# A hybrid attention block on one core: conditioning sums two weight tiles at a time, and three selection masks one to three units later

## The chip, the cores and the metric

The kernel runs on one core of a Trainium2 chip. The metric is the device time of one execution in microseconds; the figure given for a kernel is the median of several runs.

## The reference, cut to what matters

One layer of a decoder trunk with 1024 tokens and a width of 1024, all in float32:

```
mod = silu(c) W_ada + b_ada -> (shift1, scale1, gate1, shift2, scale2, gate2)
h   = RMSNorm(x) * (1 + scale1) + shift1
P   = h W_in
mixer A: out_A = u * (tril(W_s[g]) v_chunk + b[g])      # u, v = split(gelu(P_A))
mixer B: 8 query heads x 64, 2 kv heads; a light indexer scores all causal keys,
         the top 256 of them are attended with softmax
o   = concat(RMSNorm(out_A), RMSNorm(out_B)) W_out
x   = x + gate1 * RMSNorm(o)
h2  = RMSNorm(x) * (1 + scale2) + shift2
x   = x + gate2 * RMSNorm(relu(h2 W_1)^2 W_2)
```

`W_ada` is 1024 x 6144. Its first two column groups (shift1, scale1) are summed early in the kernel. The other four groups of 1024 columns are called 2 to 5 in the code: gate1, shift2, scale2 and gate2. Each is a sum over the 1024 inputs, held as eight tiles of 128 x 1024.

## The kernel before, in words

The program is written in stages: projections and the indexer first, then a selection that finds each query block's threshold among its keys, then attention, the output projection, and the feed-forward part. The code gives operations to engines by name and gives each a priority from its place in the program; a planner with a simulated timeline then fixes the order on every engine and the slots of the tile pools, and puts in the waits. Each engine runs its list in order. So an edit to the program's order moves more than the lines that it touches.

The change is in the attention stage, a loop over 32 units `u`. Query blocks of 128 tokens are taken in the order OB = 0, 7, 1, 6, 5, 4, 3, 2, four units to a block (two kv groups, two pairs of heads): units 4 to 7 are block 7, 8 to 11 block 1, 12 to 15 block 6, 16 to 19 block 5, 20 to 23 block 4, 24 to 27 block 3, 28 to 31 block 2. Block b has b + 1 key tiles, so block 1 is short work and block 6 long. In one pass of the loop the program asks for:

- `logits(u + 1)`: matmuls of queries and keys into one of three PSUM buffers (L730), a reduction on VectorE that adds the bias BI and takes the extreme (L731), and the exponential on ScalarE (L734);
- `values(u)`: transposes of the probabilities (L769), their copy by ScalarE (L750), matmuls with the values (L755), and the division by the sums on VectorE (L779, L780);
- `mask(b)` at the units listed in `MASKS`: eleven VectorE operations (L671 to L686), five of them over the block's keys, which turn the scores SC of block b into its bias BI. The mask of block b is needed at the logits of block b;
- `stack_for(u + 3)`: the queries of a coming unit (L322, L391, L392);
- `finish_a(b)` at the third unit of a block (load of the tile `ya`, VectorE L795, transposes L709, copies L712, L713), and `finish(b)` one block later for the other half (L785, L98, L99, L787, again L709 to L713);
- `WO[0] = w_chunk(...)` once: four loads of 512 KB of W_out, eight splits in two parts, on ScalarE (L224) and VectorE (L225);
- from u = 19 at odd u `oproj0`, 24 matmuls of the output projection (L807 to L809);
- `ada_sum(g)`: eight loads of W_ada (L477), and eight VectorE operations on 128 x 1024 that sum them into `adacc` (L479, L481); four units later `ada_use(g)`: sixteen matmuls with a column of ones (L165) and small VectorE operations.

Scores SC and other tiles of the selection live in pools that the loop closes at one unit; a new pool `op_` is opened in their space and holds six of the eight tiles of WO[0]. The ring `wp` has twelve slots of 4 KB a partition, for logits, queries, two tiles of WO[0], W_ada tiles and the sums. All loads named here are issued by SyncE (SP), in order.

Of the kernel before, what the change touches and what calls it, by code (L numbers as in the profile page):

```python
# [9 lines left out]
F32 = mybir.dt.float32  # L10
# [9 lines left out]
P = 128  # L20
# [3 lines left out]
KD = 8  # L24
# [13 lines left out]
def trunk(ctx, tc, x, c, positions, w_ada, b_ada, g_pre_mix, w_in, g_sgu_v, w_spatial, b_spatial,  # L38
# [8 lines left out]
    def nm(s):  # L47
        uid[0] += 1
        return f"{s}_{uid[0]}"
# [9 lines left out]
    wp = ctx.enter_context(tc.tile_pool(name="wp", bufs=12))  # L59
# [12 lines left out]
    def ct(shape, dt, name):  # L72
        return cst.tile(shape, dt, tag=name, name=name)

    def push(name, side="left"):
        st = ExitStack()
        return st, st.enter_context(tc.tile_pool(name=name, bufs=1, side=side, reuse_waits="tile"))
# [84 lines left out]
    def ada_cols(dst, acc):  # L162
        p = p_mm()
        for e in range(8):
            T.matmul(p[:, e:e + 1], acc[:, e * P:(e + 1) * P], ones, start=True, stop=True)  # L165
        V.tensor_copy(dst, p[:, :8])
# [303 lines left out]


    mod2 = ct([P, 32], F32, "mod2")
    def ada_sum(g):
        acc = wp.tile([P, 1024], F32, tag="w", name=nm("adacc"))
        for k in range(KD):
            t = wp.tile([P, 1024], F32, tag="w", name=nm("ada"))
            nc.sync.dma_start(t, w_ada[k * P:(k + 1) * P, g * 1024:g * 1024 + 1024])  # L477
            if k == 0:
                V.tensor_scalar(acc, t, cact[:, 0:1], None, op0=OP.mult)  # L479
            else:  # L480
                V.scalar_tensor_tensor(acc, t, cact[:, k:k + 1], acc, op0=OP.mult, op1=OP.add)  # L481
        return acc

    G2 = ct([P, 8], F32, "G2")
    SH2 = ct([P, 8], F32, "SH2")
# [1 line left out]
    ADA = {}  # L487

    def ada_use(g):
        m = mod2[:, (g - 2) * 8:(g - 2) * 8 + 8]  # L490
        ada_cols(m, ADA[g])
        if g == 3:
            V.tensor_tensor(SH2, m, cols[:, 32:40], op=OP.add)
        elif g == 4:
            V.scalar_tensor_tensor(G2, m, 1.0, cols[:, 40:48], op0=OP.add, op1=OP.add)
            V.tensor_tensor(G2, G2, cols[:, 56:64], op=OP.mult)
        else:
            i, b0, g0 = (0, 24, 76) if g == 2 else (1, 48, 84)
            V.tensor_tensor(gate[:, i], m, cols[:, b0:b0 + 8], op=OP.add)
            V.tensor_tensor(gate[:, i], gate[:, i], cols[:, g0:g0 + 8], op=OP.mult)  # L500
# [147 lines left out]
    def search_rest():  # L648

        V.tensor_scalar(more[:, :6], KDS, 8.0, None, op0=OP.is_gt, op1=OP.add, accum_out=more[:, 6:7])  # L650
        p = p_tr()
        flag = T.matmul(p[:1, :1], more[:, 6:7], ones, start=True, stop=True)
        V.tensor_copy(rest, p[:1, :1])
        with tc.tile_critical():
            r = V.value_load(rest)
            with V.If(r > 0):
                for b in range(2, NB):
                    cnt, sg, kk, tf, kq, lf, top8, kd, th, lo, hi = ST[b]
                    search(BI[:, boff[b]:boff[b] + P * (b + 1)].bitcast(U16), 15, lf, cnt, kd, kk, V.drain)
                V.drain()  # L660
        for b in OB[4:]:
            q_proj(b, flag)
# [3 lines left out]
    def mask(b):  # L666

        n = P * (b + 1)
        cnt, sg, kk, tf, kq, lf, top8, kd, th, lo, hi = ST[b]
        sc = score(b)  # L670
        first = V.tensor_copy(lo, lf)  # L671
        if b < 7:
            after(first, lowest[0])
        V.scalar_tensor_tensor(th, hi, 16, lo, op0=OP.logical_shift_left, op1=OP.bitwise_or)

        V.tensor_tensor(tf, th.bitcast(F32), sg, op=OP.mult)
        lt = BI[:, boff[b]:boff[b] + n]
        eq = up.tile([P, 1024], BF, tag="uv", name=nm("eq"), bufs=3)[:, :n]
        after(first, masked[0])
        V.tensor_scalar(lt, sc, tf, None, op0=OP.is_lt, op1=OP.add, accum_out=cnt)  # L680
        V.tensor_scalar(eq, sc, tf, BIG, op0=OP.is_equal, op1=OP.mult)
        V.tensor_tensor_scan(sc, eq, eq, 0.0, op0=OP.add, op1=OP.max)
        V.tensor_scalar(cnt, cnt, float(TOPK - n), BIG, op0=OP.add, op1=OP.mult)
        V.tensor_tensor(cnt, cnt, sc[:, n - 1:n], op=OP.add)
        V.scalar_tensor_tensor(eq, sc, cnt, eq, op0=OP.is_gt, op1=OP.mult)
        masked[0] = V.scalar_tensor_tensor(lt, lt, -BIG, eq, op0=OP.mult, op1=OP.subtract)  # L686
# [31 lines left out]
    def logits(u):  # L718
        b, grp, pair = units[u]
        ch = chunks(P * (b + 1))  # L720
        bias = BI[:, boff[b]:boff[b] + P * (b + 1)]
        for h2 in range(2):
            h4 = pair * 2 + h2
            h = grp * 4 + h4
            L = wp.tile([P, 1024], F32, tag="w", name=nm("L"))[:, :P * (b + 1)]
            top = 3e38
            for i, (c0, cw) in enumerate(ch):
                pl = p_lg()[:, :cw]
                for q in range(2):
                    T.matmul(pl, QS[b, grp][:, q, h4 * P:(h4 + 1) * P], KS[:, grp, c0:c0 + cw], start=q == 0, stop=q == 1)  # L730
                lowest[0] = V.tensor_tensor_reduce(L[:, c0:c0 + cw], pl, bias[:, c0:c0 + cw], scale=-0.125, scalar=top,  # L731
                                       op0=OP.add, op1=OP.min, accum_out=mxs[:, i, b, h:h + 1])
                top = mxs[:, i, b, h:h + 1]
            ex = A.activation(L, L, AF.Exp, scale=-1.0, bias=top, accum_out=sms[:, b, h:h + 1])  # L734
            after(ex, last_gelu)
            LT[u, h2] = L
# [53 lines left out]
    def finish_a(b):  # L790
        ya = p2.tile([P, 512], F32, tag="yb", name=nm("ya"), bufs=3)
        nc.sync.dma_start(ya, ya_dram[b * P:(b + 1) * P, :])
        V.tensor_tensor(rsa[:, b:b + 1], ssa[:, b, 0:1], ssa[:, b, 1:2], op=OP.add)
        rstd_of(rsa[:, b:b + 1], rsa[:, b:b + 1], 512)
        V.tensor_scalar(ya, ya, rsa[:, b:b + 1], None, op0=OP.mult)  # L795
        merge_T(b, 0, ya)

    def stack_for(u):
        if u < len(units) and units[u][2] == 0:
            b, grp, _ = units[u]  # L800
            QS[b, grp] = q_stack(p2, QT[b], grp, wp.tile([P, 2, 512], F32R, tag="w", name=nm("qs")))
# [22 lines left out]
            return op_.tile([P, 2, 512], F32R, tag="wo", name=nm("wo"), bufs=6)  # L824
        return wp.tile([P, 2, 512], F32R, tag="w", name=nm("wo"))

    MASKS = {4: 6, 6: 5, 8: 4, 9: 3, 10: 2}
    stack_for(0)
    logits(0)
    stack_for(2)  # L830
    for u, (b, grp, pair) in enumerate(units):
        if u == 3:
            at = tc.cur_priority
            tc.cur_priority = 465000
            search_rest()
            mask(7)
            tc.cur_priority = at
        if u + 1 < len(units):
            logits(u + 1)
        values(u)  # L840
        if u in MASKS:
            mask(MASKS[u])
        if u == 12:
            u_stack.close()
            sc_stack.close()
            o_stack, op_ = push("op")
        stack_for(u + 3)
        if u % 4 == 2:
            finish_a(b)
        if u in (24, 28):  # L850
            ada_use(u // 4 - 4)
        if u in (20, 24, 28):
            ADA[u // 4 - 3] = ada_sum(u // 4 - 3)
        if u % 4 == 0 and u:
            finish(OB[u // 4 - 1])
        if u == 14:
            WO[0] = w_chunk(w_out, [(0, 0, 512)], gout, tile_of=wo_tile)
        if u >= 19 and u % 2:
            oproj0(OB[(u - 19) // 2])
# [101 lines left out]
    def bank():  # L961
        nbank[0] += 1
        return BANK[(nbank[0] - 1) % 8]()
# [3 lines left out]
    def ctile():  # L967
        return fc.tile([P, 512], F32, tag="c", name=nm("c"), bufs=4)
# [133 lines left out]
    open_ = None  # L1102
    for pi in range(NF, NP):
        if pi == 5:
            ADA[5] = ada_sum(5)
        if pi == 8:
            ada_use(5)
            gate_rows(g2b, 1)
        w = wparts(pi)
        X, Y, Z = bank(), bank(), bank()  # L1110
        p1, u2, u3 = ctile(), ctile(), ctile()
        f11, f22 = dtile(), dtile()
        chained(X, w, 1, True)
        A.activation(p1, X, AF.Copy)
        if open_:
            ends(*open_)
        chained(X, w, 6, False)
        A.activation(u2, X, AF.Copy)
        chained(Z, w, 2, True)
        V.tensor_tensor(f11, p1, Z, op=OP.add)  # L1120
        relu_sq(f11, f11)
        store_x(1, pi, f11)
        chained(X, w, 7, False)
        A.activation(u3, X, AF.Copy)
        chained(Y, w, 5, True)
        V.tensor_tensor(f22, u3, Y, op=OP.add)
        relu_sq(f22, f22)
        store_x(4, pi, f22)
        open_ = (pi, w, X, Y, u2, f11, f22)
# [164 lines left out]
```

## Time and profile before

| | us |
|---|---|
| median of 3 runs | 1235.24 |
| lowest and highest of these | 1233.52, 1237.39 |
| the profiled execution, device time | 1231.81 |
| its span, first to last instruction | 1229.8 |

The profile lists, for each engine, the instructions in order of time with their durations, and marks before an instruction how long its engine was idle and which engine's work ended that. PE is TensorE's matmuls, PEld its weight loads, DVE VectorE, ACT ScalarE. "PEclk" is the granted clock of TensorE as a share of 2.4 GHz, averaged over a stretch. The attention loop runs from about 290 to 530 us of the span, its last part together with the first half of the output projection.

### The profile page before, as it was taken

To read this page: it belongs to the slowest core of one execution; us is meant where nothing else is said; L and a number is where in the kernel's file an instruction comes from. 1 tells how busy PE (TensorE), PEld (TensorE's weight loads), DVE (VectorE), ACT (ScalarE), POOL (GpSimd) and SP (SyncE) were. 2 spreads that over 40 slices of the span, in tenths; PEclk is the share of its full clock that TensorE was granted. 3 is DMA by queue.
4 is the path that set the end of the run, shared out by engine and by line. 5 is a ranking of instruction groups with operands and counts; after the bars stand their busy time and mean duration, and the time that the engine had idled before them with its cause. 6 is when DMAs were issued, how large, how long until landed. Compare 5 with 4: busy or idle time off the path is not lost.

```text
span 1229.8 us, 16884 instructions
## 1 busy us (share of the span) xinstructions
PE 1156.0 (94%) x5785; PEld 977.9 (80%) x5785; DVE 869.4 (71%) x1798; ACT 671.2 (55%) x1410; POOL 208.6 (17%) x304
## 2 busy tenths in 40 slices
PE   4899989998888999899899999999999999999997
PEld 3888768887687999787678888888887888888885
DVE  6943998995688466628997866565568656877568
ACT  4654669774367655538625555555444544445452
POOL 3585605452100000023600000000000000000001
PEclk9899999998899999899899999999999999999999
DMA  9530202110002044654226754353477365533335
GB/s 335 164 90 24 69 1 61 57 53 23 1 9 81 7 163 163 216 203 156 86 103 222 245 166 154 129 175 121 158 269 297 119 210 170 185 103 88 101 103 205
DMA packets 80240, 162.42 MB, mean 132 GB/s; under 512 B 7724, under 2 KB 32920, under 8 KB 80152
## 3 DMA queue, kind: packets, MB, share of 16 engines
q1 hardware_dynamic: 80136, 161.33, 39.1%
q8 instruction: 45, 0.74, 0.3%
q14 instruction: 43, 0.35, 0.1%
q10 hardware_dynamic: 16, 0.00, 0.0%
HBM read 119.36 MB, written 41.94 MB: 131 GB/s over the span
## 4 chain that ended last, share of the span: by engine, by line
PE 57%; DVE 10%; DMA 3%; issue 2%; ACT 2%; POOL 1%; SPq 0%; DVEq 0%; POOLq 0%; ACTq 0%
PE tr L1174 8%; PE lg L1174 8%; PE mm L1174 6%; PE mm L755 4%; PE lg L991 3%; PE lg L993 3%; PE lg L992 3%; PE tr L991 2%; PE tr L993 2%; PE tr L992 2%; PE mm L993 2%; PE mm L992 2%; PE mm L991 2%; PE tr L769 2%; PE lg L730 2%
## 5 line engine op out<-in xcount | busy, mean ns | idle before, releaser
L881 ACT ACTIVATE w<-rx 128x512 fp32r<-128x512 f32 x112 | 70.6, 631 | 147.5 <-PE lg L1174 63.8
L1174 PE MATMUL tr<-w,w 128*128 128x512 f32 x504 | 134.0, 390 | 2.1 <-DVE w L882 2.1
L1174 PE MATMUL lg<-w,w 128*128 128x512 f32 x504 | 133.8, 390 | 0.0
L882 DVE TENSOR_TENSOR w<-rx,w 128x512 fp32r<-128x512 f32 x112 | 77.1, 688 | 58.6 <-ACT w L881 58.2
L301 PE MATMUL mm<-w,hT 128*128 128x512 f32 (+1 forms) x288 | 111.8, 390 | 4.5 <-ACT hT L293 3.7
L1174 PEld LDWEIGHTS tr<-w,w 128*128 128x128 f32 x504 | 95.1, 189 | 22.3 <-DVE w L882 2.5
L1174 PEld LDWEIGHTS lg<-w,w 128*128 128x128 f32 x504 | 95.0, 189 | 19.8
L304 PE MATMUL mm<-w,hT 128*128 128x512 f32 (+1 forms) x288 | 110.1, 383 | 0.5 <-POOL hT L294 0.5
L303 PE MATMUL mm<-w,hT 128*128 128x512 f32 (+1 forms) x288 | 110.4, 384 | 0.0
L1210 POOL TENSOR_TENSOR rsf<-rsf,mhalf 128x1 f32<-128x1 f32 x8 | 6.0, 751 | 603.2 <-DVE rsf L1209 603.2
L1174 PE MATMUL mm<-w,w 128*128 128x512 f32 x336 | 94.4, 391 | 0.0
L755 PEld LDWEIGHTS mm<-VV,pT 128*128 128x128 f32 x576 | 73.7, 195 | 5.2 <-ACT pT L750 3.4
L755 PE MATMUL mm<-VV,pT 128*128 128x64 f32 x576 | 74.8, 273 | 2.0 <-ACT pT L750 2.0
L1174 PEld LDWEIGHTS mm<-w,w 128*128 128x128 f32 x336 | 63.2, 188 | 13.2
L882 DVE TENSOR_TENSOR w<-b,w 128x512 fp32r<-128x512 f32 x96 | 65.6, 684 | 3.4 <-ACT w L881 3.3
L301 PEld LDWEIGHTS mm<-w,hT 128*128 128x128 f32 x288 | 55.2, 192 | 14.0 <-ACT hT L293 3.9
L734 ACT ACTIVATE L<-L,mxs 128x128 f32<-128x128 f32 (+7 forms) x64 | 49.2, 770 | 28.3 <-DVE mxs L731 28.3
L882 DVE TENSOR_TENSOR w<-s,w 128x512 fp32r<-128x512 f32 x56 | 38.2, 687 | 36.7 <-ACT w L881 36.7
L881 ACT ACTIVATE w<-b 128x512 fp32r<-128x512 f32 x96 | 59.3, 618 | 6.4 <-DMA b<-in_w_ff_dram 6.2
L304 PEld LDWEIGHTS mm<-w,hT 128*128 128x128 f32 x288 | 54.7, 190 | 10.2 <-POOL hT L294 1.0
L730 PE MATMUL lg<-KS,qs 128*128 128x512 f32 (+5 forms) x192 | 52.2, 384 | 10.7 <-DVE mxs L731 5.7
L303 PEld LDWEIGHTS mm<-w,hT 128*128 128x128 f32 x288 | 55.2, 192 | 8.3
(356 smaller groups left out, 2964.6 us busy)
## 6 DMA issues: line engine op xcount, KB each, us to landing
rx<-x_scratch SPq DMA_DIRECT2D x56, 512.0 KB, 3.5
x_scratch<-d SPq DMA_DIRECT2D x108, 256.0 KB, 3.0
ada<-in_w_ada_dram SPq DMA_DIRECT2D x48, 512.0 KB, 5.7
raw<-in_w_ff_dram SPq DMA_DIRECT2D x32, 512.0 KB, 4.2
b<-in_w_ff_dram SPq DMA_DIRECT2D x32, 512.0 KB, 4.5
x<-in_x_dram SPq DMA_DIRECT2D x16, 512.0 KB, 5.8
raw<-in_w_in_dram SPq DMA_DIRECT2D x8, 512.0 KB, 3.6
raw<-in_w_in_dram SPq DMA_DIRECT2D x16, 256.0 KB, 2.9
```

The costliest lines, as they stand in the source:

```text
L301: mm = T.matmul(p[:, :n], lh, wt[k][:, 0, :n], start=k == 0, stop=False)
L303: T.matmul(p[:, :n], lh, wt[k][:, 1, :n], start=False, stop=False)
L304: T.matmul(p[:, :n], ll, wt[k][:, 0, :n], start=False, stop=k == KD - 1)
L730: T.matmul(pl, QS[b, grp][:, q, h4 * P:(h4 + 1) * P], KS[:, grp, c0:c0 + cw], start=q == 0, stop=q == 1)
L734: ex = A.activation(L, L, AF.Exp, scale=-1.0, bias=top, accum_out=sms[:, b, h:h + 1])
L755: mm = T.matmul(po[:, o:o + 64], e[:, (si * 2 + h2) * P:(si * 2 + h2 + 1) * P], VV[:, s0 + si, grp], start=first, stop=pair == 1 and s0 + ...
L881: A.activation(hi, src, AF.Copy)
L882: eng.tensor_tensor(lo, src, hi.bitcast(F32), op=OP.subtract)
L991: ms.append(T.matmul(p, a[:, 0, k], b[:, 0, k], start=start and k == 0, stop=False, skip_group_check=more))
L992: ms.append(T.matmul(p, a[:, 0, k], b[:, 1, k], start=False, stop=False, skip_group_check=more))
L993: ms.append(T.matmul(p, a[:, 1, k], b[:, 0, k], start=False, stop=stop and k == 3, skip_group_check=more))
L1174: ms.append(T.matmul(p, x[:, qa, t * P:(t + 1) * P], y[:, qb], start=start and n == 0, stop=stop and n == 2, skip_group_check=more))
```

## The change

Two things are edited. `MASKS` asks for the masks of blocks 4, 3 and 2 after units 9, 12 and 13 instead of 8, 9 and 10. As the scores are then needed longer, the pools of the selection close (and `op_` opens) after unit 14 instead of 12, and WO[0] is asked for at unit 15 instead of 14.

`ada_sum` becomes `ada_part(g, ks)`, which loads and sums only the tiles `ks`. In the loop, groups 2, 3 and 4 are summed two tiles a unit, in units 19 to 22, 23 to 26 and 27 to 30; before, all eight tiles were asked for at units 20, 24 and 28. `ada_use(2)` and `ada_use(3)` move from units 24 and 28 to 23 and 27. The sums of groups 2 to 4 share one slot in `op_`; before, each took a slot of `wp`. Group 5, summed in the feed-forward part, stays as it was. The number of operations and bytes is unchanged.

```diff
-    def ada_sum(g):
-        acc = wp.tile([P, 1024], F32, tag="w", name=nm("adacc"))
-        for k in range(KD):
+    def ada_part(g, ks):
+        if g not in ADA:
+            ADA[g] = (wp if g == 5 else op_).tile([P, 1024], F32, tag="w", name=nm("adacc"), bufs=12 if g == 5 else 1)
+        acc = ADA[g]
+        for k in ks:
             t = wp.tile([P, 1024], F32, tag="w", name=nm("ada"))
             nc.sync.dma_start(t, w_ada[k * P:(k + 1) * P, g * 1024:g * 1024 + 1024])
             if k == 0:
                 V.tensor_scalar(acc, t, cact[:, 0:1], None, op0=OP.mult)
             else:
                 V.scalar_tensor_tensor(acc, t, cact[:, k:k + 1], acc, op0=OP.mult, op1=OP.add)
-        return acc
...
-    MASKS = {4: 6, 6: 5, 8: 4, 9: 3, 10: 2}
+    MASKS = {4: 6, 6: 5, 9: 4, 12: 3, 13: 2}
...
-        if u == 12:
+        if u == 14:
             u_stack.close()
             sc_stack.close()
             o_stack, op_ = push("op")
         stack_for(u + 3)
         if u % 4 == 2:
             finish_a(b)
-        if u in (24, 28):
-            ada_use(u // 4 - 4)
-        if u in (20, 24, 28):
-            ADA[u // 4 - 3] = ada_sum(u // 4 - 3)
+        if u in (23, 27):
+            ada_use((u - 23) // 4 + 2)
+        if 19 <= u < 31:
+            ada_part((u - 19) // 4 + 2, range((u - 19) % 4 * 2, (u - 19) % 4 * 2 + 2))
         if u % 4 == 0 and u:
             finish(OB[u // 4 - 1])
-        if u == 14:
+        if u == 15:
             WO[0] = w_chunk(w_out, [(0, 0, 512)], gout, tile_of=wo_tile)
...
         if pi == 5:
-            ADA[5] = ada_sum(5)
+            ada_part(5, range(KD))
```

## Rows read from the trace of the kernel before

**Rows 1.** The page: busy time, share of the span and instructions of two engines.
```profile
PE 1156.0 (94%) x5785; PEld 977.9 (80%) x5785; DVE 869.4 (71%) x1798; ACT 671.2 (55%) x1410; POOL 208.6 (17%) x304
```
**Rows 2.** Stretches: length, busy PE, PEld, DVE, ACT, POOL (instructions), clock, DMA share, GB/s.
```profile
355.40:370.00 14.60, 11.34 (x82) 10.63 (x81) 12.91 (x43) 7.98 (x22) 1.77 (x3) 0.88 0.00 0
370.00:396.00 26.00, 22.33 (x167) 19.53 (x166) 23.30 (x65) 20.07 (x39) 1.90 (x3) 1.00 0.24 72
396.00:420.00 24.00, 23.52 (x201) 23.09 (x201) 13.65 (x46) 17.47 (x36) 1.77 (x3) 1.00 0.11 34
420.00:506.40 86.40, 86.40 (x594) 78.70 (x594) 54.32 (x122) 45.64 (x108) 4.23 (x7) 1.00 0.47 171
506.40:511.00 4.60, 1.18 (x10) 0.91 (x8) 4.60 (x9) 4.43 (x10) 0.00 (x0) 1.00 0.16 59
511.00:518.00 7.00, 7.00 (x24) 6.09 (x25) 3.97 (x7) 2.49 (x5) 0.00 (x0) 0.51 0.50 151
```
**Rows 3.** Timeline of PE around 361 us: start, length, line, [idle before].
```profile
360.88 0.50 PE L730 MATMUL lg<-KS,qs 128*128 128x256 f32 x2 [0.35 <-DVE mxs L731]
364.30 1.09 PE L709 MATMUL tr<-ident,yb 128*128 128x128 f32 x4 [2.91 <-DVE yb L787]
...
368.21 0.60 PE L769 MATMUL tr<-ident,L 128*128 128x128 f32 x4
```
**Rows 4.** Timeline of DVE there: the mask of block 4, and the row L787.
```profile
358.80 0.88 DVE L680 TENSOR_SCALAR_CACHE_REDUCE BI<-SC,self 128x640 bf16<-128x640 f32 x1
...
359.61 0.55 DVE L681 TENSOR_SCALAR eq<-SC,self 128x640 bf16<-128x640 f32 x1
...
361.15 1.48 DVE L682 TENSOR_TENSOR_SCAN SC<-eq 128x640 f32<-128x640 bf16 x1
...
362.87 0.88 DVE L685 SCALAR_TENSOR_TENSOR eq<-SC,self,eq 128x640 bf16<-128x640 f32 x1
363.67 0.48 DVE L787 TENSOR_SCALAR yb<-yb,rsb 128x512 f32<-128x512 f32 x1
364.06 0.82 DVE L686 SCALAR_TENSOR_TENSOR BI<-BI,eq 128x640 bf16<-128x640 bf16 x1
```
**Rows 5.** The tiles wo: matmuls and splits, ns min/median/max, first and last start.
```profile
L807 PE MATMUL mm<-wo,mT x64: 387/393/774, 421.1 to 535.6; 128*128 128x512 f32 x64
...
L224 ACT ACTIVATE wo<-raw,cols x8: 707/712/723, 382.7 to 392.3; 128x512 fp32r<-128x512 f32 x8
L225 DVE SCALAR_TENSOR_TENSOR wo<-raw,cols,wo x8: 739/747/1097, 383.7 to 394.4; 128x512 fp32r<-128x512 f32 x8
```
**Rows 6.** Timeline of PE around 509 us.
```profile
506.72 0.82 PE L769 MATMUL tr<-ident,L 128*128 128x128 f32 x6
510.96 1.11 PE L709 MATMUL tr<-ident,ya 128*128 128x128 f32 x4 [3.42 <-DVE ya L795]
```
**Rows 7.** Timeline of DVE there.
```profile
502.72 3.92 DVE L481 SCALAR_TENSOR_TENSOR adacc<-ada,cact,adacc 128x1024 f32<-128x1024 f32 x3
...
506.89 1.27 DVE L481 SCALAR_TENSOR_TENSOR adacc<-ada,cact,adacc 128x1024 f32<-128x1024 f32 x1
...
508.56 1.28 DVE L481 SCALAR_TENSOR_TENSOR adacc<-ada,cact,adacc 128x1024 f32<-128x1024 f32 x1
509.76 0.74 DVE L225 SCALAR_TENSOR_TENSOR w<-raw,cols,w 128x512 fp32r<-128x512 f32 x1
510.43 0.48 DVE L795 TENSOR_SCALAR ya<-ya,rsa 128x512 f32<-128x512 f32 x1
```
**Rows 8.** The W_ada tiles of 420 to 530 us: issues, waits, landing.
```profile
L477 SPq DMA_DIRECT2D ada<-in_w_ada_dram x24: 327/371/740, 431.6 to 499.3; - x24
...
  DMA ada<-in_w_ada_dram: 3.1, 3
...
DMA to landing us min/median/max: 3.7/5.9/7.5
```
**Rows 9.** Timeline of PE: the first twelve of one ada_use's sixteen matmuls.
```profile
468.28 1.45 PE L165 MATMUL mm<-ones,adacc 128*128 128x1 f32 x12
```

## What bounds the kernel now, and what the change should do to it

> **What bounds the kernel now.** The page's first part comes first: the matmul row of TensorE is busy for 94% of the span, VectorE for 71% [rows 1]. Such a kernel ends when TensorE has done its list, so only two things can make it shorter: gaps in TensorE's row, and time at the lower of its two clock levels. The 40 slices point to the attention loop, and the view by stretches shows where in it [rows 2]. From 355.4 to 370 us (the tail of block 7 and block 1) TensorE is idle for 14.60 - 11.34 = 3.26 us, and the mean granted clock is 0.88. With levels of 1.2 and 2.4 GHz that mean says that 24% of the stretch, 3.5 us, ran at half speed, which cost about 1.75 us. From 370 to 396 (block 6) it is idle for 3.67 us at full clock; from 396 to 420 (block 5) for 0.48; from 420 to 506.4 for nothing, though VectorE has 32 us free there. Then 3.42 us idle in 506.4 to 511, and 7.00 us at a clock of 0.51, so about 3.4 us lost: 6.8 us together.
>
> Then the timelines, for what ends those gaps. The first big one, 2.91 us, ends with VectorE's L787 of `finish(7)` [rows 3]. VectorE was never idle: L787 stands behind the scan and L685 of block 4's mask [rows 4]. After that gap four transposes take 1.09 us, and only at 368.21 are they back at 0.60 [rows 3]: this is the low clock. The second gap, 3.42 us, ends with L795 of `finish_a(2)` [rows 6], and before L795 VectorE did five steps of the sum of group 4 and a weight split with hardly a pause [rows 7]. So in both places TensorE waits for a short VectorE operation that stands in line behind long ones nobody needs yet. From 370 to 396 VectorE is busy for 23.30 of 26.0 us [rows 2]; eight splits of WO[0] are part of that [rows 5].
>
> **The change part by part.** Nothing is removed or added: 24 sums, 24 loads and five masks stay. All that moves is place, so every term below is a share of idle time that exists now. The profiled execution took 1231.8 us (span 1229.8, and 2.0 around it), 3.4 under the median of 1235.2; the gain is worked out on the first and taken off the second.
>
> *Block 1's stretch.* The mask of block 4 costs 0.88 + 0.55 + 1.48 + 0.88 + 0.82 = 4.6 us for its five long steps [rows 4] and some 0.8 more for six small ones. It is asked for one unit later, behind `finish(7)`. The mask of block 3 (0.8 of the keys) leaves the stretch; its first three long steps fell into it, by scaling 0.8 x 2.91 = 2.3 us, and some small ones, about 3 together. VectorE then has 12.91 - 3 = 9.9 us of work here, and TensorE needs 11.34 - 1.75 = 9.6 at full clock. Ends: no gain at all (block 4's mask of 5.4 us is still one burst amid short units) and 14.6 - 9.9 = 4.7 us. I take the middle, **2.4**, as the burst stays but its victim `finish(7)` is gone.
>
> *Block 6's stretch.* In come 3 us of block 3's mask, out go the eight VectorE splits, 8 x 0.747 = 6.0 us [rows 5]: 23.3 + 3 - 6 = 20.3 us of VectorE against 22.3 of TensorE [rows 2]. It fits in sum, but both masks stand in the first half. Ends 0 and 3.67; I take half, **1.8**.
>
> *Block 5's stretch.* WO[0]'s splits, one unit later, fall mostly into it: ScalarE 17.47 + 8 x 0.712 = 23.2 us of 24.0, VectorE 13.65 + 6.0 = 19.7 [rows 2, 5]. ScalarE's copies feed the values' matmuls, so a nearly full ScalarE will show. Ends: nothing, and 2.9 us, most of the idle time that block 6 has with these splits now. I take **-1.5**. The loads of WO[0] on SP move with it, behind the `ya` load of unit 14 as before; first use is at unit 19, and the last split now starts at 394.4 and the first matmul with these tiles at 421.1 [rows 5], so a shift of a unit costs nothing there.
>
> *Units 19 to 27.* Two sums a unit, 2.6 us at most, in a stretch where VectorE has 32 of 86 us free [rows 2]: no gain and no loss; the cover is that free time. What is new here are two waits. First, loads come in twelve pairs instead of three sets of eight. Three sets cost VectorE 3.1 us of waiting for a landing [rows 8]; twelve would cost 12, still inside the free time. Behind a wait for a load stand L731 of the next logits, and TensorE behind that. On SP the pairs stand between the `ya` loads and the stores of `oproj0`, and an issue that waits for a slot of `wp` holds these up. Sums no longer take slots there, and at most a few W_ada tiles are open at once, so I count nothing for it. Second, the sums of groups 2 to 4 share one slot: the first sum of group 3 must wait until sixteen L165 matmuls have read group 2, and likewise for 4. Twelve of them take 1.45 us [rows 9]; L731, L780 and L713 queue behind. TensorE has a unit's worth of values and 24 matmuls of `oproj0` to go on with, so again nothing in the sum, with 0 as one end and the last rival's price as the other.
>
> *The end of the loop.* At unit 30 two sums stand where five stood before L795: 3 x 1.28 = 3.8 us less ahead of it [rows 7], more than the gap of 3.42 [rows 6]. If the gap goes the low clock goes with it. Ends 0 and 6.8; VectorE may put other early work there, as it did with the split L225 [rows 7], so I take **5.0**. What is late next is `finish(2)`, whose transposes have `oproj0` and stage 8's projection to cover them; the later stages just start earlier.
>
> Sum: 2.4 + 1.8 - 1.5 + 5.0 = **7.7 us**. The profiled execution would come to 1224.1, the median to 1235.2 - 7.7 = **1227.5**.
>
> **The rivals.**
>
> *The masks only move their stall* (blocks 1 and 6 give nothing, block 5 costs 1.5): for it, VectorE is the full engine from 355 to 396 and its work there hardly shrinks; against it, the rows show one victim, not a lack of capacity. 5.0 - 1.5 = 3.5 us: 1231.7.
>
> *The end keeps its gap*, since what stands before L795 is decided by the planner, which already put a stage-8 split there [rows 7]. Only 2.7 us are won: 1232.5.
>
> *Everything comes back*: 4.7 + 3.7 + 6.8 = 15.2 us, 1220.0. For it, all the gaps have one cause; against it, bursts of 4 to 5 us remain.
>
> *Spread gaps keep the clock low.* Instead of one gap of 2.9 us, TensorE gets several short ones, and half speed remains. In this trace gaps of 3.67 us in all, none with a fall behind it, left the clock at 1.00 from 370 to 396 [rows 2], which speaks against it. Price: the 1.75 us of block 1 stay and block 6 loses as much: 7.7 - 3.5 = 4.2 us, 1231.0. The Trainium skill (TensorE: Matmul & The Clock Gate, section "A second HAM failure mode: psum-queue depth-cycling") describes this: frequent short idles between groups of matmuls make the clock swing. The trace so far doesn't agree.
>
> *Slower: the shared slot of the sums.* At units 23 and 27 VectorE stands at the first sum of the next group until TensorE, which is behind in its own list, has reached L165. If that lasts longer than what TensorE can do without VectorE (the values of one unit and an `oproj0`), TensorE runs dry and its clock falls, as around 509 us: 6.8 us each time, 13.6 for two. 13.6 - 7.7 = 5.9 us slower: 1241.1. Against it: TensorE has no gap at all there now and the wait is a few us.
>
> **How the numbers follow.** Forecast 0.40 (own range 1223 to 1231), stall moved 0.19, end stays 0.13, everything 0.09, clock 0.05, slower 0.14. Faster by over 0.3% (3.7 us, about what a measurement of this kernel can tell from no change) is below 1231.5: the forecast, "everything", half of "stall moved", half of "clock": 0.40 + 0.09 + 0.095 + 0.025 = 0.61. Slower 0.14, the rest, 0.25, is the same. The range from 1220 to 1238 leaves out the slower case and half of "everything".
>
> **What would show it.** Right: no gap over 2 us before L709 in block 1 and at the end, full clock in both places, and VectorE's busy share near even from 420 to 510. Block 5's term: ScalarE's L750 ending gaps in TensorE just after WO[0]'s loads. Wrong: a gap of 3 us or more with a fall of the clock anywhere from 356 to 530, above all one that ends with L481, L479 or L165 (the shared slot or late loads), or a new one ahead of L795. If the time is the same and TensorE's idle time has shrunk, it was given back behind the loop, in stage 8, where VectorE and ScalarE lead.

## The result and the profile after

The changed kernel took **1225.41 us** (median of four executions, 1224.78 to 1229.68), the kernel before 1234.38 beside it: a ratio of **0.9939, 95% interval 0.9918 to 0.9961**. Run again as an experiment below, it gave 0.9955 [0.9938, 0.9972]. By these two ratios the change is worth some 5.5 to 7.5 us; 7.7 were forecast, and 1225.41 is 2.1 below the predicted 1227.5.

The profiled execution of the changed kernel is the slowest of its four, 1229.68 with a span of 1227.9. Its busy times [rows 1] are the same work:

```profile
PE 1156.1 (94%) x5785; PEld 977.7 (80%) x5785; DVE 870.3 (71%) x1798; ACT 671.3 (55%) x1410; POOL 210.9 (17%) x304
```

The view by stretches, with the columns of [rows 2]:

```profile
355.00:370.00 15.00, 12.06 (x98) 11.02 (x98) 12.26 (x36) 8.26 (x23) 2.43 (x3) 1.00 0.00 0
370.00:396.00 26.00, 25.93 (x208) 24.83 (x206) 25.58 (x78) 21.90 (x43) 1.78 (x3) 1.00 0.08 18
396.00:420.00 24.00, 22.77 (x181) 21.68 (x182) 15.14 (x44) 18.52 (x38) 1.78 (x3) 1.00 0.29 93
...
450.00:480.00 30.00, 28.26 (x181) 25.27 (x179) 16.53 (x33) 12.25 (x30) 1.78 (x3) 0.94 0.43 139
480.00:506.00 26.00, 24.50 (x158) 21.75 (x156) 23.56 (x44) 15.53 (x40) 0.55 (x1) 1.00 0.69 223
506.00:520.00 14.00, 12.47 (x80) 11.14 (x81) 5.94 (x10) 9.70 (x21) 2.29 (x2) 1.00 0.51 156
```

Two numbers come out of each line: TensorE's idle time (length less busy PE), and what the low clock costs, (1 - clock) x length. This holds since half speed for a time T loses T/2 and lowers the mean by as much. From 450 to 480 that is 1.74 idle and 0.06 x 30 = 1.8. The table adds them up for every kernel, idle time + clock.

| profiled execution | 355-370 | 370-396 | 396-420 | 420-480 | 480-520 | lost | loop |
|---|---|---|---|---|---|---|---|
| before | 3.3+1.7 | 3.7+0 | 0.5+0 | 0+0 | 3.4+3.4 | 15.9 | 288.5 |
| after | 2.9+0 | 0.1+0 | 1.2+0 | 1.7+1.8 | 3.0+0 | 10.8 | 283.9 |
| e3_same | 2.9+0 | 0.3+0 | 0.7+0 | 1.7+5.1 | 3.0+1.8 | 15.7 | 287.7 |
| e1_masks_only | 2.9+0 | 0.3+0 | 0.7+0 | 0+0 | 2.6+3.4 | 9.9 | 282.4 |
| e2_sums_only | 3.3+2.7 | 2.9+0.8 | 1.3+0 | 1.7+1.8 | 2.7+0 | 17.1 | 290.7 |
| e4_sums_in_eights | 2.9+0 | 0.4+0 | 0.8+0 | 0.5+1.8 | 3.4+3.4 | 13.1 | 286.5 |
| e5_masks_wo_at_14 | 2.9+0 | 1.5+0 | 0.9+0 | 0+0 | 2.8+1.8 | 10.0 | 283.2 |
| e6_two_slots | 2.9+0 | 0.2+0 | 1.1+0 | 1.7+1.8 | 3.0+3.5 | 14.3 | 287.0 |
| e7_sums_two_earlier | 2.9+0 | 0.4+0 | 1.0+0 | 3.4+6.6 | 4.3+4.8 | 23.3 | 300.3 |
| e8_ya_first | 2.9+0 | 0.3+0 | 0.7+0 | 1.1+1.8 | 4.8+9.6 | 21.3 | 294.6 |
| e9_mask4_only | 2.9+0 | 1.6+1.8 | 0.5+0 | 0+0 | 2.6+3.4 | 12.7 | 285.1 |
| e10_masks32_only | 3.3+1.7 | 1.0+0 | 1.8+3.4 | 0+0 | 3.2+3.4 | 17.6 | 288.9 |
| e11_masks_ya_first | 2.9+0 | 0+0 | 1.2+0 | 0+0 | 3.7+1.7 | 9.5 | 282.6 |
| e12_masks_sums_18 | 2.9+0 | 0.3+0 | 0.9+0 | 0+1.8 | 3.0+3.5 | 12.4 | 284.7 |

"Loop" is read from the timeline of PE: from the end of the idle time that block 7's mask causes (L730 at 315.88 before) to the end of the first one of stage 8 (L904 at 604.33 before). "Loop" less "lost" is 271.3 to 273.6 for all but e7, whose clock stays low past 520. So the list of gaps and falls (spells at the lower clock) accounts for the loop to some 2 us. Idle times repeat to half a microsecond between the two profiles of one program (after, e3_same); the clock's share does not.

Outside the loop, where no edit lies, the profiled executions scatter: against before they are between 2.2 us shorter and 1.2 longer ahead of it, and between 2.1 shorter and 4.4 longer behind it. The profile of after, 4.6 us shorter in the loop, is only 1.9 shorter in its span; that of e1, 6.0 shorter in the loop, is 8.8 shorter. So the ratios of the timed executions, and not one profile, say what a version is worth.

The gaps of the changed kernel, timeline of PE (start, length, what, idle before and its releaser; line numbers are one or two higher than before's):

```profile
363.41 0.63 PE L710 MATMUL tr<-ident,yb 128*128 128x128 f32 x4 [1.84 <-DVE self L684]
...
368.44 1.10 PE L756 MATMUL mm<-VV,pT 128*128 128x64 f32 x8 [0.79 <-ACT pT L751]
...
452.54 0.66 PE L710 MATMUL tr<-ident,ya 128*128 128x128 f32 x4 [1.74 <-DVE ya L796]
...
484.10 0.63 PE L710 MATMUL tr<-ident,ya 128*128 128x128 f32 x4 [0.67 <-DVE ya L796]
...
486.23 0.63 PE L322 MATMUL tr<-ident,qd 128*128 128x128 f32 x4 [0.63 <-DVE mT L714]
...
506.56 0.66 PE L770 MATMUL tr<-ident,L 128*128 128x128 f32 x4 [0.76 <-DVE mT L714]
...
509.64 1.52 PE L756 MATMUL mm<-VV,pT 128*128 128x64 f32 x12 [0.96 <-DVE yb L781]
```

Beside [rows 3], the gap of 2.91 us ahead of block 1's transposes is now 1.84, and the transposes take 0.63 us instead of 1.09: no fall of the clock. Beside [rows 6], the 3.42 us ahead of L709 are gone, and several short gaps stand there, at full clock. The third line is new.

The gap in block 1 shrank in an unforeseen way. Timeline of VectorE, beside [rows 4]:

```profile
361.51 0.88 DVE L681 TENSOR_SCALAR_CACHE_REDUCE BI<-SC,self 128x640 bf16<-128x640 f32 x1
...
362.32 0.55 DVE L682 TENSOR_SCALAR eq<-SC,self 128x640 bf16<-128x640 f32 x1
362.78 0.48 DVE L788 TENSOR_SCALAR yb<-yb,rsb 128x512 f32<-128x512 f32 x1
...
363.24 1.48 DVE L683 TENSOR_TENSOR_SCAN SC<-eq 128x640 f32<-128x640 bf16 x1
```

The planner still starts block 4's mask ahead of `finish(7)`, but the short L788 now goes in before the scan and L686, where before it stood behind both.

The new gap, timeline of VectorE:

```profile
449.49 1.28 DVE L483 SCALAR_TENSOR_TENSOR adacc<-ada,cact,adacc 128x1024 f32<-128x1024 f32 x1
450.68 0.17 DVE L780 RECIPROCAL sms<-sms 128x4 f32<-128x4 f32 x1
450.80 1.28 DVE L483 SCALAR_TENSOR_TENSOR adacc<-ada,cact,adacc 128x1024 f32<-128x1024 f32 x1
452.00 0.48 DVE L796 TENSOR_SCALAR ya<-ya,rsa 128x512 f32<-128x512 f32 x1
```

and what TensorE does behind it:

```profile
453.91 1.84 PE L165 MATMUL mm<-ones,adacc 128*128 128x1 f32 x16
455.61 1.98 PE L756 MATMUL mm<-VV,pT 128*128 128x64 f32 x16
...
458.94 0.63 PE L809 MATMUL mm<-wo,mT 128*128 128x512 f32 x1
...
461.77 0.39 PE L808 MATMUL mm<-wo,mT 128*128 128x512 f32 x1
```

Two sums stand in line ahead of L796 of `finish_a(4)`, though TensorE needs their result only at L165, behind the transposes that wait for L796: the pattern of [rows 7], 58 us earlier in the span. A little later a matmul of 512 columns takes 0.63 us instead of 0.39, the lower clock level.

The gap at the end of the loop went in an unforeseen way too. The last sum ends at 505, but L796 of `finish_a(2)` starts no earlier for it: its load is issued at 507.64 us, where it was 499.71 before, and VectorE waits for that.

```profile
511.87 0.49 DVE L796 TENSOR_SCALAR ya<-ya,rsa 128x512 f32<-128x512 f32 x1 [2.38 <-DMA ya<-ya_scratch]
```

TensorE isn't held up, since its list now has matmuls of `oproj0` there, from 510.97 to 515.40, ahead of the transposes. In e2, e3 and e6 below it is the same.

### The profile page after: what moved, and what is told of

It is laid out like the page before. It is cut to its first block, busy times and chain, and to the rows that moved or that the text cites. A ratio compares the mean times of both kernels' runs of the same rounds, so it can differ in the third digit from the quotient of the medians.

```text
span 1227.9 us, 16880 instructions
## 1 busy us (share of the span) xinstructions
PE 1156.1 (94%) x5785; PEld 977.7 (80%) x5785; DVE 870.3 (71%) x1798; ACT 671.3 (55%) x1410; POOL 210.9 (17%) x304
## 4 chain that ended last, share of the span: by engine, by line
PE 60%; DVE 8%; ACT 2%; DMA 2%; issue 2%; POOL 1%; POOLq 0%; DVEq 0%; SPq 0%; ACTq 0%
PE lg L1175 9%; PE tr L1175 9%; PE mm L1175 6%; PE mm L756 4%; PE lg L992 3%; PE lg L994 3%; PE lg L993 3%; PE tr L992 2%; PE tr L994 2%; PE tr L993 2%; PE tr L770 2%; PE lg L731 2%; PE mm L992 2%; PE mm L994 2%; PE mm L993 2%
```

## The experiments

Ratios are to the kernel before on the same chip, with 95% intervals. e1 to e4 ran on one chip, e8 to e11 on a second, and e5, e6, e7 and e12 on a third, so numbers of different groups are compared by their ratios.

**e1_masks_only**: the masks, the pools and WO[0] as in the change, the sums as before.

```diff
-    MASKS = {4: 6, 6: 5, 8: 4, 9: 3, 10: 2}
+    MASKS = {4: 6, 6: 5, 9: 4, 12: 3, 13: 2}
...
-        if u == 12:
+        if u == 14:
...
-        if u == 14:
+        if u == 15:
```

> Only the masks, the pools' closing and WO[0] are moved; the sums stay eight at a time at units 20, 24 and 28. My theory (two separate gains): the stall at 361 us shrinks and the clock stays up there, the gap of some 3.4 us before L795 at the end of the loop stays with its half clock; 2.7 us faster than before, about 1231.5. Rival 'the masks only move their stall': no change or 1.5 us slower. Rival 'the masks are all of it': 9 us faster, as the whole change measured.

Measured: 1227.22, ratio **0.9934 [0.9922, 0.9947]**. This half alone gives the whole gain, as far as the intervals can tell; 2.7 us were expected and 8.1 came. Its gaps in blocks 1, 6 and 5 are those of the change, and 420 to 480 is clean; the end is not:

```profile
450.00:480.00 30.00, 30.00 (x202) 26.95 (x202) 20.03 (x42) 16.95 (x41) 1.83 (x3) 1.00 0.46 167
480.00:506.00 26.00, 23.44 (x156) 21.15 (x155) 19.03 (x36) 14.69 (x36) 0.55 (x1) 0.93 0.52 193
506.00:520.00 14.00, 13.97 (x76) 11.99 (x76) 4.69 (x9) 6.23 (x13) 1.83 (x2) 0.89 0.52 170
```

**e2_sums_only**: the other half, with `ada_part` as in the change.

```diff
-        if u in (24, 28):
-            ada_use(u // 4 - 4)
-        if u in (20, 24, 28):
-            ADA[u // 4 - 3] = ada_sum(u // 4 - 3)
+        if u in (23, 27):
+            ada_use((u - 23) // 4 + 2)
+        if 19 <= u < 31:
+            ada_part((u - 19) // 4 + 2, range((u - 19) % 4 * 2, (u - 19) % 4 * 2 + 2))
```

> Only the sums go two tiles a unit with one shared slot outside the ring; masks, pools and WO[0] as before. My theory: the gap before L795 at the end and its 7 us of half clock go, the gap of 2.9 us at 361 us and its half clock stay; 5 to 6 us faster than before, about 1229. Rival 'the sums are all of it': 9 us faster. Rival 'the shared slot costs': a gap of TensorE that ends with L481 or L165 near units 23 and 27, and less than 3 us gained.

Measured: 1234.15, ratio **0.9993 [0.998, 1.0006]**: nothing clear of noise, where 5 to 6 us were expected. The gap of block 1 is the old one, and the new gap of 1.74 us is there:

```profile
364.27 0.69 PE L710 MATMUL tr<-ident,yb 128*128 128x128 f32 x4 [2.91 <-DVE yb L788]
...
458.65 0.66 PE L710 MATMUL tr<-ident,ya 128*128 128x128 f32 x4 [1.74 <-DVE ya L796]
```

In the table it wins 4.1 us from 480 to 520 and loses 3.5 from 420 to 480: what the sums bring at the end of the loop they take at unit 22.

**e3_same**: the changed kernel itself, beside the two.

> The whole change unaltered, as the reference for its parts on this chip and for a second profile. My theory: 9 us faster than before, and a profile that differs from the first, which had a clock of 0.975 against 0.978 of its three other executions, in where the clock is low: the half-clock spell after 456 us is missing or shorter. Rival: the spell is part of the change and comes back in every profile, and then the timed runs carry it too.

Measured: 1230.55 (nine executions, 1225.11 to 1234.08), 0.9955 [0.9938, 0.9972]; its interval overlaps that of e1. Its profile has the gaps of "after" and another clock:

```profile
450.00:480.00 30.00, 29.23 (x161) 26.55 (x161) 13.89 (x29) 9.88 (x24) 1.17 (x2) 0.83 0.39 125
```

0.17 x 30 = 5.1 us were lost there instead of 1.8, behind the same list of instructions. So the expectation that the spell would be missing or shorter failed, and its rival held.

**e4_sums_in_eights**: the change, but all eight tiles of a group asked for at its first unit. This parts "in pairs" from "one unit earlier".

```diff
-        if 19 <= u < 31:
-            ada_part((u - 19) // 4 + 2, range((u - 19) % 4 * 2, (u - 19) % 4 * 2 + 2))
+        if u in (19, 23, 27):
+            ada_part((u - 19) // 4 + 2, range(KD))
```

> The changed kernel, but each group's eight tiles asked for at once at units 19, 23 and 27; the shared slot outside the ring and the uses at 23 and 27 stay. My theory (a burst of sums ahead of L795 is what costs): a gap of 2 us or more before an L795 or L788 returns with a fall of the clock; 4 to 6 us slower than the whole change. Rival 'what helps is the ring slot that the sums give up, or starting one unit earlier': same time as the whole change, within 1.5 us.

Measured: 1230.23, 0.9963 [0.9949, 0.9978], the same as the change within the intervals, where 4 to 6 us slower had been expected. So pairs are worth nothing over eights that these runs can tell. The big gap before L796 is gone (0.5 us idle in all from 420 to 480), yet the clock fell there.

**e8_ya_first**: the change, with the last two sums of group 2 ordered behind L795 (here L800) of `finish_a(4)`, to remove the new gap.

```diff
+                if g == 2 and k >= 6:
+                    after(s, ya_op[0])
...
-        V.tensor_scalar(ya, ya, rsa[:, b:b + 1], None, op0=OP.mult)
+        ya_op[0] = V.tensor_scalar(ya, ya, rsa[:, b:b + 1], None, op0=OP.mult)
```

> The whole change, with one order written in: the last two sums of group 2 stand behind L795 of finish_a(4) on VectorE instead of one of them ahead of it. My theory (the sums' gain at the end is given back by a new gap of 1.74 us before L795 near 450 us and the half clock that follows the sixteen matmuls of ada_use): the gap there goes to some 0.5 us, the clock stays at 1.00, and the kernel is 3 to 5 us faster than the whole change, about 1226 where that measured 1230.5. Rival 'the late load holds L795 (an issue of a W_ada tile ahead of it on SP waits for a slot)': the gap stays, VectorE waits for ya's landing, no change.

Measured: 1233.93, 0.9989 [0.9973, 1.0005]: the gain of the change is lost. The gap shrank where it was meant to, from 1.74 to 0.48 us, and the same pattern came 30 us later, in `finish_a(3)`:

```profile
483.71 1.00 PE L714 MATMUL tr<-ident,ya 128*128 128x128 f32 x4 [2.11 <-DVE ya L800]
```

Timeline of VectorE there:

```profile
480.59 2.58 DVE L485 SCALAR_TENSOR_TENSOR adacc<-ada,cact,adacc 128x1024 f32<-128x1024 f32 x2
483.08 0.48 DVE L800 TENSOR_SCALAR ya<-ya,rsa 128x512 f32<-128x512 f32 x1
```

Behind it lay a clock of 0.74 for 26 us. That sums in line before L795 make the gap is shown; that its removal helps is not, since it moved.

**e9_mask4_only** and **e10_masks32_only** split e1: the first moves block 4's mask (and, by one unit each, those of blocks 3 and 2), with pools, WO[0] and sums as before; the second leaves block 4's where it was and moves the rest of e1.

```diff
-    MASKS = {4: 6, 6: 5, 8: 4, 9: 3, 10: 2}
+    MASKS = {4: 6, 6: 5, 9: 4, 10: 3, 11: 2}
```

> Kernel before with only the mask of block 4 moved behind finish(7) (units 9, 10, 11 for the three masks; pools, WO[0] and sums as before). My theory: the gap before L709 at 361 us goes from 2.9 to some 1.8 us, the clock stays up after it; block 6 keeps 3 to 4 us of idle time; 2 us faster than before. Rival 'it is all the clock': 5 us or more. Rival 'block 6 is all of it': no change.

```diff
-    MASKS = {4: 6, 6: 5, 8: 4, 9: 3, 10: 2}
+    MASKS = {4: 6, 6: 5, 8: 4, 12: 3, 13: 2}
...
-        if u == 12:
+        if u == 14:
...
-        if u == 14:
+        if u == 15:
```

> Only the masks of blocks 3 and 2 move (units 12 and 13), with the pools' closing and WO[0]; the mask of block 4 stays at unit 8, ahead of finish(7). My theory: the gap of 2.9 us at 361 us and its half clock stay, TensorE's idle time in block 6 falls from 3.7 us to under 0.5; 3 to 4 us faster than before. Rival 'it is all block 1': no change. Rival 'the full VectorE just moves': block 6 keeps its idle time.

Measured: 0.9957 [0.994, 0.9975] and 0.9973 [0.9957, 0.9988]. The product, 0.9930, is e1's 0.9934: the two add up. e9 gained 5.3 us where 2 were expected: the number of its rival "it is all the clock". Block 1 is that of the change, and half of block 6's idle time goes (1.8 us of low clock come in there, behind a gap of 1.18 us). Its profile is 3.4 us shorter in the loop and 4.2 in the span, so some 1 us of the 5.3 isn't in that profile. In e10 the old gap stands, and block 6 gains 2.6 us:

```profile
364.18 1.06 PE L709 MATMUL tr<-ident,yb 128*128 128x128 f32 x4 [2.90 <-DVE yb L787]
```

Its profile also shows a fall in block 5 after a gap of 1.39 us, so that it gains nothing over before in the table; the timed executions say 0.27%.

**e11_masks_ya_first**: e1 with the last three sums of group 4 ordered behind L795 of `finish_a(2)`, aimed at the gap at the end.

```diff
+        if u == 30:
+            ada_sum(4, range(5, KD))
...
+                if ks[0]:
+                    after(s, ya_op[0])
```

> Only the masks, pools and WO[0] moved as in the change; sums eight at a time as before except the last group, whose last three are asked for after L795 of finish_a(2) and ordered behind it. My theory: the gap of 2.3 us before L795 at the end, seen with the masks alone, shrinks below 1 us and the clock stays up from 480 to 520; 3 us faster than the masks alone, about 1224, and faster than the whole change. Rival 'weight splits or the load take the sums' place ahead of L795': same as the masks alone, about 1227.

Measured: 1228.67, 0.9947 [0.9928, 0.9966], no better than e1. The gap ahead of L709 went, and one of 3.15 us behind ScalarE's copy came:

```profile
515.49 1.90 PE L759 MATMUL mm<-VV,pT 128*128 128x64 f32 x12 [3.15 <-ACT pT L754]
```

**e5_masks_wo_at_14**: e1 with WO[0] at unit 14, as before. **e6_two_slots**: the change with two slots for the sums instead of one.

```diff
-        if u == 15:
+        if u == 14:
             WO[0] = w_chunk(w_out, [(0, 0, 512)], gout, tile_of=wo_tile)
```

> The masks and pools moved as in the change, sums as before, WO[0] asked for at unit 14 as before. My theory: its splits then meet the masks of blocks 3 and 2 in block 6, and TensorE's idle time there (3.7 us before, 0.3 with WO[0] at 15) returns to 1.5 to 3 us: 2 us slower than the masks alone, 0.995 of before. Rival 'only the masks matter, WO[0] is hidden at either place': 0.993 of before, as the masks alone.

```diff
-            ADA[g] = (wp if g == 5 else op_).tile([P, 1024], F32, tag="w", name=nm("adacc"), bufs=12 if g == 5 else 1)
+            ADA[g] = (wp if g == 5 else op_).tile([P, 1024], F32, tag="w", name=nm("adacc"), bufs=12 if g == 5 else 2)
```

> The whole change with two slots instead of one for the sums of groups 2 to 4. My theory: the wait for the shared slot is never last, so the gaps near 450 and 485 to 515 us stay as in the whole change and the time is the same within 1.5 us, 0.994 to 0.996 of before. Rival 'the shared slot costs what the split sums should have gained': 3 us or more faster than the whole change, 0.992 of before or less.

Measured: 0.9965 [0.9946, 0.9984] and 0.9953 [0.9937, 0.9969]. The first hints that WO[0]'s unit is worth some 4 us with the masks moved (e1 has 0.9934, and the intervals just touch); in the profiles the loop differs by 0.8 us, so it stays a hint. The second equals e3_same, and its idle times are those of the change nearly everywhere: the shared slot costs nothing.

**e7_sums_two_earlier**: the change with the pairs at units 17 to 28 and the uses at 21 and 25.

```diff
-        if u in (23, 27):
+        if u in (21, 25):
...
-        if 19 <= u < 31:
+        if 17 <= u < 29:
```

> The whole change with the pairs of sums two units earlier (units 17 to 28, uses at 21 and 25). My theory: pairs of sums make short gaps ahead of an L795 wherever they land, so one of some 1.5 us with a spell of half clock comes back in another place; 0.994 to 0.997 of before. Rival 'the end of the loop is short of VectorE time, and sums away from it give the gain': gaps from 480 to 520 us fall below 1 us in all and it is 3 us faster than the whole change, 0.992 of before.

Measured: 1241.49, **1.0056 [1.0035, 1.0078]**, slower than before, which neither the expectation nor its rival had. The sums now meet the short operations of other blocks:

```profile
435.67 1.37 PE L731 MATMUL lg<-KS,qs 128*128 128x320 f32 x4 [1.18 <-DVE mxs L732]
...
472.78 0.63 PE L710 MATMUL tr<-ident,yb 128*128 128x128 f32 x4 [2.02 <-DVE yb L788]
...
516.37 0.65 PE L770 MATMUL tr<-ident,L 128*128 128x128 f32 x4 [3.21 <-DVE mT L714]
```

Timeline of VectorE ahead of the last of them: a weight split put into the time that the sums left.

```profile
513.64 2.07 DVE L225 SCALAR_TENSOR_TENSOR w<-raw,cols,w 128x512 fp32r<-128x512 f32 x3
515.63 0.68 DVE L714 TENSOR_TENSOR mT<-tr,mT 128x512 fp32r<-128x512 f32 x1
```

**e12_masks_sums_18**: e1 with the sums in eights at units 18, 22 and 26 and the uses at 22 and 26.

```diff
-        if u in (24, 28):
-            ada_use(u // 4 - 4)
-        if u in (20, 24, 28):
-            ADA[u // 4 - 3] = ada_sum(u // 4 - 3)
+        if u in (22, 26):
+            ada_use((u - 22) // 4 + 2)
+        if u in (18, 22, 26):
+            ADA[(u - 18) // 4 + 2] = ada_sum((u - 18) // 4 + 2)
```

> The masks, pools and WO[0] moved as in the change; sums eight at a time, but at units 18, 22 and 26 (uses at 22 and 26), so that none is left for the last units. My theory now (TensorE's last units lack work that doesn't wait, and something else stands ahead of L795 when the sums are gone): about 3 us of idle time stay between 480 and 520 us; 0.993 of before, as the masks alone. Rival 'the sums cause the gap at the end': less than 1 us idle there and 0.990 of before.

Measured: 1227.38, 0.9958 [0.9939, 0.9976]. Idle time is e1's within 0.5 us, but the clock fell also at both uses of the sums, at 450 and at 482 us. The first of these falls has no gap of 0.6 us or more ahead of it. Timeline of PE:

```profile
448.14 1.00 PE L755 MATMUL mm<-VV,pT 128*128 128x64 f32 x8
448.98 1.90 PE L165 MATMUL mm<-ones,adacc 128*128 128x1 f32 x16
450.74 0.90 PE L709 MATMUL tr<-ident,ya 128*128 128x128 f32 x4
451.43 0.85 PE L769 MATMUL tr<-ident,L 128*128 128x128 f32 x3
```

and the stretch: PE busy throughout at a clock of 0.62.

```profile
450.00:454.00 4.00, 4.00 (x25) 4.00 (x26) 2.79 (x6) 1.20 (x2) 0.00 (x0) 0.62 1.02 400
```

In e9, as in before, the planner put eight matmuls of the values between twelve and four L165 matmuls, and the clock stayed at 1.00:

```profile
465.33 1.45 PE L165 MATMUL mm<-ones,adacc 128*128 128x1 f32 x12
466.64 1.08 PE L755 MATMUL mm<-VV,pT 128*128 128x64 f32 x8
467.56 0.56 PE L165 MATMUL mm<-ones,adacc 128*128 128x1 f32 x4
467.98 0.63 PE L709 MATMUL tr<-ident,yb 128*128 128x128 f32 x4
```

No version here beats e1 or the changed kernel beyond the intervals.

## Why the prediction was right, and where its steps were not

The total is right: 7.7 us forecast; 7.5 by the ratio of the first measurement, 5.5 by that of the repetition (9.0 and 4.2 by their medians). That it is so near is luck. By the halves timed alone, the masks gave 8.1 us where their three terms come to 2.7, and the sums gave 0.9 where 5.0 were forecast; the two errors nearly cancel. Every cost below is read from the profiles, as idle time and clock.

*Block 1, 2.4 forecast.* By the table 4.9 - 2.9 = 2.0 us, in every kernel that has the mask moved. The size was right, but only 0.3 of it is idle time; 1.7 is the low clock, which is gone. "Its victim `finish(7)` is gone" was half right: the mask still starts first, the gap is 1.84.

*Block 6, 1.8 forecast.* 3.6 in the profile of after, 3.3 in e1 and e3. Undersized: half was taken because both masks stand in the first half, and TensorE showed no gap from that.

*Block 5, -1.5 forecast.* -0.2 to -0.8. The mechanism is the one named: the three gaps of after there (0.34, 0.58 and 0.38 us) all end with ScalarE's L751. They are shorter than feared. The three mask terms together gave 4.8 to 5.1 in the profiles of e1, after and e3. What e1's timing has beyond that is in part 0.8 us at the end of the loop; the rest lies outside the loop or is chance.

***Units 19 to 27, "no gain and no loss": the step that failed.*** The cover named was VectorE's 32 free us. Free time in the sum is no cover for a short operation that stands in line at the wrong moment, which is just what [rows 4] and [rows 7] had shown elsewhere. The pairs put sums ahead of L795 of `finish_a(4)`: 1.74 us idle, the same in after, e2, e3 and e6. It is a new gap ahead of an L795, which the prediction itself named as a sign of being wrong. The uses moved too, and the text priced L165 at its time alone (1.45 us for twelve [rows 9]) and not at the low clock that came beside it. Cost: 3.5 us in after, e2 and e6, 6.8 in e3. Nor did the pairs make VectorE's work even: its busy share is 0.60, 0.55 and 0.91 in 420 to 450, 450 to 480 and 480 to 506, where before had 0.61, 0.64 and 0.63.

Of the two waits that the text feared there, that for the shared slot was harmless (e6), and so was that for the tiles. The first sum of a group now waits for nothing; the view of VectorE's lines of after from 420 to 530 us (count | busy us, mean ns | idle before) has

```profile
L481 DVE TENSOR_SCALAR adacc<-ada,cact 128x1024 f32<-128x1024 f32 x3 | 2.2, 750 | 0.0
```

where the sums of before waited 3.1 us for landings [rows 8], 2.6 of them ahead of a first sum; and the 24 tiles land in 4.6 us (median) against 5.9. What came late is the `ya` load, whose wait of 2.4 us TensorE covered.

*The end of the loop, 5.0 forecast.* L795's gap went, but not as worked out: it was to go because fewer sums stand ahead of L795, and what removed it is that TensorE has other matmuls while L795 comes later. And 3.0 us of idle time stay between 480 and 520 in four short pieces, against 3.4; the two last end with `mT` and `yb`, which stand behind weight splits. What was won is the clock, and not in every profile: 3.4 us in after and e2, 1.5 in e3, nothing in e6. Together with units 19 to 27 the sums give nothing clear of noise (e2).

*The rivals.* "The masks only move their stall" fell (e1), and "everything comes back" fell with the first measurement. "The end keeps its gap" holds for e1, and nearly for the change: idle time moved, not removed. "Slower: the shared slot" fell (e6). "Spread gaps keep the clock low" fell for blocks 1 and 6, where after, e1 and e3 have a clock of 1.00. At the end of the loop it is open: the gaps of 0.76 and 0.96 us stand in after, e2, e3 and e6, and in e6 alone a fall follows them (512 to 515 us). The Trainium skill (TensorE: Matmul & The Clock Gate, "A second HAM failure mode: psum-queue depth-cycling") describes a clock that swings with frequent short idles; one of these four profiles may agree, three do not.

*Not settled.* Whether L165 lowers the clock, or its neighbours too, was not tried in isolation. Of e9's 5.3 us its profile shows 2.0 in block 1, 0.3 in block 6, 0.8 at the end of the loop and 0.8 outside it; the rest is open too.

## What to carry to other kernels

Before you spread optional work over "free" time of an in-order engine, look for the short operations of that engine on which the bound engine waits, and see what stands ahead of each: a gap removed in one place came back at another such operation in e2, e7 and e8, and behind ScalarE in e11. Time each half of a change alone; here one half gave the whole gain, and the other half looked good only in the stretch that it was meant for. And check what fills the bound engine's row, not only that it is full.

## What the runs showed of the hardware

**A full row of PE can still lose its clock.** In e12 PE shows no idle time at all from 420 to 480 us, and still the clock is 0.62 from 450 to 454. That is beside the first use of the sums in the loop (sixteen one-column matmuls). With this use at unit 21, 22 or 23, eight profiles (after, e2, e3, e4, e6, e7, e8, e12) all have a fall beside it. In four of them (e4, e7, e8, e12) no gap over 1.2 us stands ahead, in e12 none of 0.6. With the use at unit 24, six profiles (before, e1, e5, e9, e10, e11) have no fall there. One fall costs about 1.7 us in most, 5.1 in e3.

That the sixteen stand undivided is not the whole cause. They do so in seven of the eight, and are split 12 and 4 in the six without a fall; but e8 has them split 12 and 4 too, by four matmuls of 64 columns, and falls. And at their third use, at 518 to 537 us amid 512-column matmuls, they stand undivided in all fourteen profiles, with a clock of 1.00 behind them in each.

**The same list may or may not fall.** At the second use, the PE rows of after and e3 agree from L165 on (sixteen, two transposes, six matmuls of the logits). In after the matmuls that follow take 0.39 us, in e3 0.63. So do e9 and e1 at their second use, 12 and 4 in both: 1.00 in e9, and in e1 the clock 0.58 from 492 to 496. The Trainium skill (TensorE: Matmul & The Clock Gate, "What's actually happening") says that the gate's watch runs free of the kernel's start, so that its place varies from run to run; these pairs fit that, but don't show it. This may be part of a spread of 9 us over nine executions of one program (e3_same), though the mean clock doesn't explain it: 0.977 in the fastest of the nine, 0.976 in the slowest. It is why terms under 2 us are better read from idle times than from one profile's clock.

**A gap's length alone doesn't tell.** A gap of 1.41 us at 387 us left the clock at 1.00 in before; one of 1.39 in e10 at 400 was followed by a mean of 0.86 in that block, and one of 1.18 in e9 at 373 by 0.59 from 374 to 378. The gap of 2.9 us in block 1 was followed by a fall in three of three profiles, that of 1.84 in none of eleven.
